# A Transformer block with gated linear attention on one core: every pair of a down pass by sums, with the sums kept over the rounds

## The chip, the cores and the metric

The kernel runs on one core of one Trainium2 chip. The metric is the device time of one execution in microseconds, as the median of several runs. TensorE is called PE below, VectorE DVE, ScalarE ACT, GpSimd POOL, and SyncE, which issues most transfers, SP.

## The reference

One layer for 256 tokens of 2048 values: a mixer with gated linear attention, then a multilayer perceptron (MLP) with a squared ReLU, each ahead of a residual addition and behind an RMS norm, and a last RMS norm.

```python
h = x
h = h + _gla_mixer(_rmsnorm(h, gla_norm), gla_w_in, gla_w_gate_up, gla_b_gate, gla_o_norm, gla_w_out)
h = h + _sq_relu_mlp(_rmsnorm(h, mlp_norm), mlp_w_up, mlp_w_down)
return _rmsnorm(h, final_norm)

def _sq_relu_mlp(h, w_up, w_down):     # w_up 2048 x 8192, w_down 8192 x 2048
    a = jax.nn.relu(h @ w_up)
    return (a * a) @ w_down
```

The change bears on the product with `w_down`, and on how the normed input of the mixer lies in SBUF.

## The kernel before

**Arithmetic.** Every large matrix is float32. A float32 factor is split into a high part (a cast to the type fp32r, done on ACT) and a low part (the difference, done on DVE), and a product is three matmuls: high by high, high by low, low by high. A matmul is 128 x 128 by 256 columns. `halves` (L146) issues those of most stages, `turned` (L180) those in which the weights are the stationary factor.

**Weights.** `weights` loads 128 rows of a weight matrix by SP into a buffer `raw` (three pairs of rows), and splits them into a slot `hi` and a slot `lo` (`parts`, L109 and L110; for `turned` L134 and L135). There are five slots of each, so the splitting runs ahead of PE by at most five slices of 1024 columns.

**Stages.** First come the products of the mixer, the gate, the scores and the output product. Then the MLP, in `ROUNDS` = 4 rounds of 2048 hidden values each: a round has four calls of `up` (q from 0 to 3), which make 512 hidden values each and leave them in `act`, and `down` for the left half of the output columns (half 0) and the right half (half 1). The right half of the last round is done by a closing loop instead, plain, which also ends the kernel.

**The MLP's `up`.** After the 192 matmuls of a call, DVE applies the ReLU (L620), ACT squares (L624), DVE makes four sums of blocks (L627), and both split the result into `act` (L632, L633).

**The MLP's `down`.** A call (a *pass*) has eight pairs of 128 hidden values by 1024 output columns. Of these columns the right 512 are always done plainly, into two banks of PSUM (`plain`). The left 512 columns are seen as 2 x 2 blocks (two halves of the hidden pair by two halves of the columns), and the tokens as two halves as well. A pair *by sums* takes seven block products in place of eight, in Strassen's manner: sums of blocks of `act` (S1 to S4, made in `up`) meet sums of blocks of the weights, made by three operations on DVE (L683) into `work` and split like a third slice `wu`. The seven products go to six half-banks, `b32`, `b74`, `b16`, `b50`. The first pair of a pass (`PLAIN = (0,)`) is done plainly, into the plain banks and parts of the same four. At the end of a pass `take` (L639) adds banks to h, and the combination of the products is made in `ends` (L703, L704) and added to h (L713).

**Order.** PE, DVE and ACT work off their own instruction lists, written out ahead of time by a scheduler that places each instruction by a simulated timeline. So the instructions of a pass's end, of the tail of an up call and of the splitting of the next weights stand mixed on DVE and ACT. Smaller work is put into a list `side` and issued between weight slices by `pump`.

**Where operands lie.** A stationary operand starts 48 values into a block of 64 (`OFF`), a moving one at its start. In each stage that needs it, one row or slice (`EVEN`, `xe`, `gap`) is stored at the other offset. The normed input x, split and turned, lies in two tiles `xth` and `xtl` of 16 rows of 320 values each (`ROW`); behind each row its first 16 values are repeated (`wrap_input`), so that a row can be read from value 16 on when it is the moving operand (`xts`). The tiles that hold the turned h later (`hth`, `htl`) reuse their place.

Of the kernel before, what the change touches and what calls it, by code (L numbers as in the profile page):

```python
# [56 lines left out]
WRAP = 16  # L57
ROW = 320
OFF = 48
EVEN = 5  # L60
# [6 lines left out]
def tile_gla_mlp(ctx, tc, x, xt, cols, w_vg, w_in, w_gate, w_out, w_up, w_down, final_norm, out):  # L67
# [99 lines left out]

    def turned(ah, al, w, c0, even=(0,), acc=None):

        acc = acc or acc_banks(GT // P // 2)  # L170
        for kp in range(KT // 2):
            wh, wl = weights(w[2 * kp * P : 2 * (kp + 1) * P, c0 : c0 + GT].rearrange("(i p) c -> p i c", p=P), 2 * GT, gap=kp in even)
            for i in range(2):
                kt = 2 * kp + i
                for j in range(GT // P):
                    s = slice(j * P, (j + 1) * P)
                    o = acc[j // 2][:, j % 2 * T : (j % 2 + 1) * T]
                    for n, (u, m) in enumerate(((wh, ah), (wh, al), (wl, ah))):

                        nc.tensor.matmul(  # L180
                            o, u[:, i, s], m[:, kt], start=kt == 0 and n == 0 and j % 2 == 0,
                            stop=kt == KT - 1 and n == 2, skip_group_check=True,
                        )
                if kt < KT - 1:
                    pump()
        return acc
# [18 lines left out]
    for _ in range(WARM):  # L205
# [10 lines left out]
    kab = big.tile([P, 2, 8, T], F32, tag="C", name="kab")  # L216
    xth, xtl = (
        big.tile([P, KT * ROW + 64], F32R, tag="A" + i, name="x" + i, bufs=1)[:, OFF : OFF + KT * ROW]
        .rearrange("p (k t) -> p k t", t=ROW)
        for i in "hl"  # L220
    )
    xts = [a[:, :, WRAP : WRAP + T] for a in (xth, xtl)]

    xe = mid.tile([P, 2, P], F32R, tag="xe", name="xe")

    def row_x(kt, t):
        if kt == EVEN and t == 0:
            return [xe[:, i] for i in range(2)]
        return [a[:, kt, t * P : (t + 1) * P] for a in (xth, xtl)]

    def wrap_input(lo, hi):
        k = slice(lo, hi)
        nc.scalar.copy(xth[:, k, T : T + WRAP], xth[:, k, :WRAP].bitcast(F32))
        nc.vector.tensor_copy(xtl[:, k, T : T + WRAP], xtl[:, k, :WRAP].bitcast(F32))

# [12 lines left out]
    def input_tile(kt):  # L248
        if kt in x_loads:
            s = slice(x_done[0], x_loads[kt])  # L250
            nc.sync.dma_start(out=xr[:, s, :], in_=xv[:, s, :])  # L251
            x_done[0] = x_loads[kt]
        if kt == KT - 1:
            wrap_input(0, KT - 2)
        nc.scalar.activation(xth[:, kt, :T], xr[:, kt, :], AF.Copy, scale=g1(kt))  # L255
        nc.vector.scalar_tensor_tensor(
            xtl[:, kt, :T], xr[:, kt, :], g1(kt), xth[:, kt, :T].bitcast(F32), op0=ALU.mult, op1=ALU.subtract
        )
        if kt == EVEN:
            nc.scalar.copy(xe[:, 0], xth[:, kt, :P].bitcast(F32))  # L260
            nc.vector.tensor_copy(xe[:, 1], xtl[:, kt, :P].bitcast(F32))
        return [(0, 512), (512, WMAX)] if kt < FINE else None
# [62 lines left out]
    flush()  # L325
    wrap_input(KT - 2, KT)
    for t in range(NT):
# [89 lines left out]
    for half in range(2):  # L417
        acc = turned(*xts, w_in, KEYW + half * GT, even=(0,) if half else (2,), acc=None if half else [aux_bank(), aux_bank()])
        for b in range(2):
            c0 = 4 * half + 2 * b  # L420
            from_bank(kab[:, 0, c0 : c0 + 2], acc[b])
# [15 lines left out]
    for half in range(2):  # L437
        acc = turned(*xts, w_in, half * GT, even=())
        for b in range(2):
            c0 = 4 * half + 2 * b  # L440
            from_bank(qt[:, c0 : c0 + 2], acc[b])
        side.extend([lambda c=c: extend_q(c) for c in range(4 * half, 4 * half + 4)])
# [131 lines left out]
    add_h(acc, 0)  # L574
    hth, htl = (big.tile([P, KT, T], F32R, tag="A" + i, name="h" + i, bufs=1) for i in "hl")
    turned_h = lambda kt: [a[:, kt, :].rearrange("p (t s) -> p t s", t=NT) for a in (hth, htl)]
    side.extend([lambda: None] + [lambda q=q: turn(h, turned_h, g2, q) for q in range(4)])
# [33 lines left out]
    work = work[:, : 3 * G].rearrange("p (b c) -> p b c", b=3)  # L611
    ends = mid.tile([P, 4, T], F32, tag="db", name="ends")

    def up(r, q, act):
        acc = turned(hth, htl, w_up, r * D + q * GT, even=() if q > 1 or r > 0 and q else (5,) if r == q == 0 else (0,))
        flush()
# [21 lines left out]
    def take(bank, t, lo, n):  # L638
        nc.vector.tensor_tensor(h[:, t, lo : lo + n], bank, h[:, t, lo : lo + n], op=ALU.add)  # L639

    PLAIN = (0,)

    def down(r, half, act):
# [3 lines left out]
        b32, b74 = acc_banks(2) if half == 0 else [aux_bank(), aux_bank()]  # L647
        b16, b50 = acc_banks(2)
        left, right = slice(0, T), slice(T, 2 * T)
        used = set()  # L650

        def product(bank, o, a, w, m, last):

            for i, (x, y) in enumerate(((0, 0), (0, 1), (1, 0))):
                halves(bank[:, o], a[x], w[y][:, m], bank.name not in used, last and i == 2)
                used.add(bank.name)

        for kp in range(KP):
# [5 lines left out]
            ]  # L664
            if kp in PLAIN:
                for i in range(2):
                    wi = weights(w(2 * kp + i), G)
                    blocks(i, wi)
                    product(b32, slice(0, 512), at(A11 + i), wi, slice(0, 512), False)
                    product(b50, right, at(A21 + i), wi, left, False)  # L670
                    product(b74, right, at(A21 + i), wi, right, False)
                    pump()
                continue
            assert not raw_half
# [17 lines left out]
            blocks(1, w1)  # L692
            product(b50, left, at(S1), wu, slice(0, T), last)
            product(b74, left, at(S3), wu, slice(T, 2 * T), last)
# [7 lines left out]

        tt = lambda o, x, y: nc.vector.tensor_tensor(o, x, y, op=ALU.subtract)  # L703
        nc.scalar.copy(ends[:, 1], b16[:, left])  # L704
        tt(ends[:, 3], ends[:, 1], b16[:, right])
        tt(ends[:, 0], b50[:, left], ends[:, 3])
        tt(ends[:, 2], ends[:, 3], b74[:, left])
        take(b32, 0, c0, 512)
        take(b74, 1, c0, 512)
        take(b50[:, right], 1, c0, T)  # L710
        for t in range(NT):
            hv = h[:, t, c0 : c0 + 512].rearrange("p (i s) -> p i s", i=2)
            nc.vector.tensor_tensor(hv, hv, ends[:, 0 : t + 2 : t + 1], op=ALU.add)  # L713

# [105 lines left out]
```

## Time and profile before

| | us |
|---|---|
| median of 3 runs | 1073.5 (1072.7 to 1073.9) |
| the profiled execution, its own time | 1072.98 |
| its span, first to last instruction | 1071.1 |
| busy: PE, DVE, ACT, POOL | 1061.8, 775.1, 574.2, 12.7 |
| granted TensorE clock | 0.998 of full speed |

Times are microseconds from the start of the span. A row of a timeline has start, duration, engine, line, operation, tiles (out<-in), shapes and count, and in brackets the idle time of the engine just before and what ended it. A row of the waits has total, times and longest. A row of the windows has a stretch, its length, the busy time of PE, of PE's weight loading, of DVE, ACT and POOL (each with a count), the granted clock, the share of the DMA engines and GB/s. A row of the groups has line, engine, operation, tiles, shapes and count, then busy time in us, mean ns of one, and idle time before. Matmuls are pipelined, so a matmul is shown as 0.28 us long while the next starts 0.11 us after it.

### The profile page before, as it was taken

What the parts mean: (1) busy time and instruction counts of PE and PEld (TensorE: products, weight loads), DVE (VectorE), ACT (ScalarE), POOL (GpSimd) and SP (SyncE); (2) the same over time, 40 slices, a digit from 0 to 9 for tenths busy, and PEclk for the clock granted to TensorE, in tenths of its full rate; (3) what the DMA queues carried; (4) which work ended last, traced back from release to release, by engine and by line L of the source; (5) the groups of instructions that cost most, each with busy time, mean ns of one, the idle gap of its engine ahead of it and who ended that gap; (6) DMA issues with size and microseconds to landing.
All of it is one profiled execution on the core that took longest, in us unless ns stands there. A gap on an engine that the chain in (4) does not pass through costs nothing.

```text
span 1071.1 us, 21851 instructions
## 1 busy us (share of the span) xinstructions
PE 1061.8 (99%) x9283; PEld 1060.9 (99%) x9283; DVE 775.1 (72%) x1026; ACT 574.2 (54%) x693; POOL 12.7 (1%) x39
## 2 busy tenths in 40 slices
PE   9999999999999999999999999999999999999997
PEld 9999999999999999999999999999999999999997
DVE  7677654656555566789986689987779997678874
ACT  7675444546445455555555446564555554555552
POOL 0000000000000000000000000000000000000000
PEclk9999999999999999999999999999999999999999
DMA  9847654655555555555576555566655656665662
GB/s 341 305 157 233 196 185 137 178 151 179 197 183 183 186 179 183 194 190 201 197 227 204 191 194 173 195 223 210 197 197 179 213 200 215 191 194 189 205 228 79
DMA packets 79569, 210.43 MB, mean 196 GB/s; under 512 B 6720, under 2 KB 7616, under 8 KB 79344
## 3 DMA queue, kind: packets, MB, share of 16 engines
q1 hardware_dynamic: 78512, 206.99, 58.6%
q10 hardware_dynamic: 960, 2.05, 0.5%
q8 instruction: 72, 1.18, 0.4%
q14 instruction: 25, 0.20, 0.1%
HBM read 206.92 MB, written 2.10 MB: 195 GB/s over the span
## 4 chain that ended last, share of the span: by engine, by line
PE 96%; DMA 1%; issue 1%; ACT 0%; DVE 0%; SPq 0%; POOLq 0%; POOL 0%; DVEq 0%; ACTq 0%
PE acc L146 42%; PE acc L180 39%; PE aux L146 12%; PE aux L180 2%; DMA zz<-in_xt 1%; PE aux L525 1%; PE aux L454 1%; DMA raw<-in_w_vg 0%; ACT xh L255 0%; SPq L138 0%; DVE lo L110 0%; ACT hi L109 0%; PE acc L355 0%; SPq L251 0%; DVE hf L779 0%
## 5 line engine op out<-in xcount | busy, mean ns | idle before, releaser
L110 DVE TENSOR_TENSOR lo<-raw,hi 128x1024 fp32r<-128x1024 f32 (+2 forms) x225 | 258.5, 1151 | 123.2 <-ACT hi L109 122.2
L109 ACT CAST hi<-raw 128x1024 fp32r<-128x1024 f32 (+2 forms) x225 | 223.4, 994 | 214.9 <-PE acc L146 115.5
L180 PE MATMUL acc<-hh,hi 128*128 128x256 f32 x1024 | 283.2, 277 | 0.0
L180 PE MATMUL acc<-hh,lo 128*128 128x256 f32 x1024 | 283.1, 276 | 0.0
L180 PE MATMUL acc<-hl,hi 128*128 128x256 f32 x1024 | 283.0, 276 | 0.0
L135 DVE TENSOR_TENSOR lo<-raw,hi 128x1024 fp32r<-128x1024 f32 x160 | 195.7, 1224 | 115.3 <-ACT hi L134 114.6
L134 ACT CAST hi<-raw 128x1024 fp32r<-128x1024 f32 x160 | 168.1, 1051 | 187.5 <-PE acc L180 144.7
L146 PE MATMUL acc<-hi,act 128*128 128x256 f32 x1202 | 217.3, 276 | 0.0
L180 PEld LDWEIGHTS acc<-hh,hi 128*128 128x128 f32 x1024 | 192.3, 188 | 0.0
L180 PEld LDWEIGHTS acc<-hh,lo 128*128 128x128 f32 x1024 | 192.3, 188 | 0.0
L180 PEld LDWEIGHTS acc<-hl,hi 128*128 128x128 f32 x1024 | 192.3, 188 | 0.0
L146 PEld LDWEIGHTS acc<-hi,act 128*128 128x128 f32 x1202 | 180.2, 188 | 0.0
L146 PE MATMUL acc<-lo,act 128*128 128x256 f32 x601 | 142.1, 276 | 0.0
L146 PE MATMUL aux<-hi,act 128*128 128x256 f32 x716 | 135.1, 276 | 0.0
L146 PEld LDWEIGHTS aux<-hi,act 128*128 128x128 f32 x716 | 107.9, 188 | 0.0
L146 PEld LDWEIGHTS acc<-lo,act 128*128 128x128 f32 x601 | 101.9, 188 | 0.0
L146 PE MATMUL acc<-lo,xh 128*128 128x256 f32 x496 | 79.7, 279 | 0.1
L146 PE MATMUL acc<-hi,xh 128*128 128x256 f32 x496 | 78.7, 281 | 0.3 <-ACT hi L109 0.3
L146 PE MATMUL acc<-hi,xl 128*128 128x256 f32 x496 | 78.8, 278 | 0.0
L146 PE MATMUL aux<-lo,act 128*128 128x256 f32 x358 | 76.9, 276 | 0.0
L109 ACT CAST hi<-work 128x1024 fp32r<-128x1024 f32 x49 | 51.7, 1055 | 32.0 <-PE aux L146 12.0
L146 PEld LDWEIGHTS acc<-hi,xh 128*128 128x128 f32 x496 | 66.7, 188 | 0.8 <-ACT hi L109 0.7
(147 smaller groups left out, 1386.1 us busy)
## 6 DMA issues: line engine op xcount, KB each, us to landing
raw<-in_w_up SPq DMA_DIRECT2D x128, 512.0 KB, 4.5
raw<-in_w_down SPq DMA_DIRECT2D x128, 512.0 KB, 4.4
raw<-in_w_in SPq DMA_DIRECT2D x80, 512.0 KB, 4.6
raw<-in_w_out SPq DMA_DIRECT2D x32, 512.0 KB, 4.3
raw<-in_w_vg SPq DMA_DIRECT2D x13, 520.0 KB, 8.0
h<-in_x SPq DMA_DIRECT2D x4, 512.0 KB, 7.1
zz<-in_xt SPq DMA_DIRECT2D x3, 384.0 KB, 7.5
fb<-in_final_norm ACTq DMA_DIRECT2D x1, 1024.0 KB, 7.0
```

What stands on the lines that cost most here:

```text
L109: last_hi[0] = nc.scalar.copy(hi[:, s], raw[:, s])
L110: last_lo[0] = nc.vector.tensor_tensor(lo[:, s], raw[:, s], hi[:, s].bitcast(F32), op=ALU.subtract)
L134: last_hi[0] = nc.scalar.copy(to[0], dst)
L135: last_lo[0] = nc.vector.tensor_tensor(to[1], dst, to[0].bitcast(F32), op=ALU.subtract)
L146: nc.tensor.matmul(o[:, m], x, w[:, m], start=first and c == 0, stop=last, skip_group_check=True)
L180: nc.tensor.matmul(o, u[:, i, s], m[:, kt], start=kt == 0 and n == 0 and j % 2 == 0, stop=kt == KT - 1 and n == 2, skip_group_check=True,)
L454: nc.tensor.matmul(o, kab[:, k[0], c0 + c, k[1] : k[1] + P], q(qt[:, c0 + c]), start=c == 0, stop=c == 1)
L525: nc.tensor.transpose(b[:, i * T + t * P : i * T + (t + 1) * P], src[:, t, kt * P : (kt + 1) * P], ident)
```

## The change

All eight pairs of a pass are done by sums; the branch for the plain pair goes. The bank `b50`, whose right half only the plain pair used, becomes `b5`, half used; likewise the left half of `b74` now holds only the product with the sums S3, and only its right half is added to h.

The combination is no longer made at the end of every pass. Two new tiles `sums`, one for each half of the columns, hold four blocks. In round 0 ACT copies the banks `b16`, `b5` and the left half of `b74` there; in later rounds DVE adds them on. In the last pass of each half (round 3 for half 0, round 2 for half 1) the four blocks are combined once and added to h.

The room for `sums` comes from the input: x's high and low part are each cut into a tile of 12 rows (`CUT`), whose place the turned h takes later, and one of 4 rows, whose place `sums` takes. `turned` now gets a function that gives a row. The wrapped columns are copied for rows 0 to 11 before the last row is made, and for rows 12 to 15 after the stage, where it was 0 to 13 and 14 to 15.

```diff
+CUT = 12
-    def turned(ah, al, w, c0, even=(0,), acc=None):
+    def turned(row, w, c0, even=(0,), acc=None):
...
+                ah, al = row(kt)
...
-                            o, u[:, i, s], m[:, kt], start=kt == 0 and n == 0 and j % 2 == 0,
+                            o, u[:, i, s], m, start=kt == 0 and n == 0 and j % 2 == 0,
...
+    xs = [
+        [
+            big.tile([P, n * ROW + 64], F32R, tag=k + i, name="x" + k, bufs=1)[:, OFF : OFF + n * ROW].rearrange("p (k t) -> p k t", t=ROW)
+            for i in "hl"
+        ]
+        for k, n in (("A", CUT), ("E", KT - CUT))
+    ]
+    def x_row(kt, lo, hi):
+        return [a[:, kt - CUT * (kt >= CUT), lo:hi] for a in xs[kt >= CUT]]
...
         if kt == KT - 1:
-            wrap_input(0, KT - 2)
+            wrap_input(0, 0, CUT)
...
-    wrap_input(KT - 2, KT)
+    wrap_input(1, 0, KT - CUT)
...
+    sums = [big.tile([P, 4, T], F32, tag="E" + i, name="sums", bufs=1) for i in "hl"]
...
-    PLAIN = (0,)
...
-        b16, b50 = acc_banks(2)
+        b16, b5 = acc_banks(2)
...
-            if kp in PLAIN:
-                for i in range(2):
-                    wi = weights(w(2 * kp + i), G)
-                    blocks(i, wi)
-                    product(b32, slice(0, 512), at(A11 + i), wi, slice(0, 512), False)
-                    product(b50, right, at(A21 + i), wi, left, False)
-                    product(b74, right, at(A21 + i), wi, right, False)
-                    pump()
-                continue
...
-        tt = lambda o, x, y: nc.vector.tensor_tensor(o, x, y, op=ALU.subtract)
-        nc.scalar.copy(ends[:, 1], b16[:, left])
-        tt(ends[:, 3], ends[:, 1], b16[:, right])
-        tt(ends[:, 0], b50[:, left], ends[:, 3])
-        tt(ends[:, 2], ends[:, 3], b74[:, left])
+        e = sums[half]
         take(b32, 0, c0, 512)
-        take(b74, 1, c0, 512)
-        take(b50[:, right], 1, c0, T)
+        if r == 0:
+            nc.scalar.copy(e[:, 1:3].rearrange("p b c -> p (b c)"), b16)
+            nc.scalar.copy(e[:, 0], b5[:, left])
+            nc.scalar.copy(e[:, 3], b74[:, left])
+        else:
+            both = e[:, 1:3].rearrange("p b c -> p (b c)")
+            nc.vector.tensor_tensor(both, b16, both, op=ALU.add)
+            nc.vector.tensor_tensor(e[:, 0], b5[:, left], e[:, 0], op=ALU.add)
+            nc.vector.tensor_tensor(e[:, 3], b74[:, left], e[:, 3], op=ALU.add)
+        take(b74[:, right], 1, c0 + T, T)
+        if r < ROUNDS - 1 - half:
+            return
+
+        tt = lambda o, x, y, op: nc.vector.tensor_tensor(e[:, o], e[:, x], e[:, y], op=op)
+        tt(2, 1, 2, ALU.subtract)
+        tt(0, 0, 2, ALU.subtract)
         for t in range(NT):
+            if t == 1:
+                tt(1, 2, 3, ALU.subtract)
+                tt(0, 0, 3, ALU.add)
             hv = h[:, t, c0 : c0 + 512].rearrange("p (i s) -> p i s", i=2)
-            nc.vector.tensor_tensor(hv, hv, ends[:, 0 : t + 2 : t + 1], op=ALU.add)
+            nc.vector.tensor_tensor(hv, hv, e[:, :2], op=ALU.add)
```

More of the change, by code (lines that the diff above doesn't have):

```diff
@@ L216, in tile_gla_mlp @@
     kab = big.tile([P, 2, 8, T], F32, tag="C", name="kab")
[L217 to L222, printed above, removed]
+    xs = [
[7 more added lines that the diff above has]
+        return [a[:, kt - CUT * (kt >= CUT), lo:hi] for a in xs[kt >= CUT]]
+    stream_x = lambda kt: x_row(kt, WRAP, WRAP + T)
     xe = mid.tile([P, 2, P], F32R, tag="xe", name="xe")
@@ L228, in row_x, with wrap_input @@
             return [xe[:, i] for i in range(2)]
[L229 to L234, printed above, removed]
+        return x_row(kt, t * P, (t + 1) * P)
+    def wrap_input(part, lo, hi):
+        h, l = (a[:, lo:hi] for a in xs[part])
+        nc.scalar.copy(h[:, :, T : T + WRAP], h[:, :, :WRAP].bitcast(F32))
+        nc.vector.tensor_copy(l[:, :, T : T + WRAP], l[:, :, :WRAP].bitcast(F32))
     def from_bank(dst, bank):
@@ L253, in input_tile @@
         if kt == KT - 1:
-            wrap_input(0, KT - 2)
[L255 to L258, printed above, removed]
+            wrap_input(0, 0, CUT)
+        h, l = x_row(kt, 0, T)
+        nc.scalar.activation(h, xr[:, kt, :], AF.Copy, scale=g1(kt))
+        nc.vector.scalar_tensor_tensor(l, xr[:, kt, :], g1(kt), h.bitcast(F32), op0=ALU.mult, op1=ALU.subtract)
         if kt == EVEN:
-            nc.scalar.copy(xe[:, 0], xth[:, kt, :P].bitcast(F32))
-            nc.vector.tensor_copy(xe[:, 1], xtl[:, kt, :P].bitcast(F32))
+            nc.scalar.copy(xe[:, 0], h[:, :P].bitcast(F32))
+            nc.vector.tensor_copy(xe[:, 1], l[:, :P].bitcast(F32))
         return [(0, 512), (512, WMAX)] if kt < FINE else None
@@ L417, in tile_gla_mlp @@
     for half in range(2):
-        acc = turned(*xts, w_in, KEYW + half * GT, even=(0,) if half else (2,), acc=None if half else [aux_bank(), aux_bank()])
+        acc = turned(stream_x, w_in, KEYW + half * GT, even=(0,) if half else (2,), acc=None if half else [aux_bank(), aux_bank()])
         for b in range(2):
@@ L437, in tile_gla_mlp @@
     for half in range(2):
-        acc = turned(*xts, w_in, half * GT, even=())
+        acc = turned(stream_x, w_in, half * GT, even=())
         for b in range(2):
@@ L611, in tile_gla_mlp @@
     work = work[:, : 3 * G].rearrange("p (b c) -> p b c", b=3)
-    ends = mid.tile([P, 4, T], F32, tag="db", name="ends")
     def up(r, q, act):
-        acc = turned(hth, htl, w_up, r * D + q * GT, even=() if q > 1 or r > 0 and q else (5,) if r == q == 0 else (0,))
+        acc = turned(lambda kt: (hth[:, kt], htl[:, kt]), w_up, r * D + q * GT, even=() if q > 1 or r > 0 and q else (5,) if r == q == 0 else (0,))
         flush()
@@ L692, in down @@
             blocks(1, w1)
-            product(b50, left, at(S1), wu, slice(0, T), last)
+            product(b5, left, at(S1), wu, slice(0, T), last)
             product(b74, left, at(S3), wu, slice(T, 2 * T), last)
```

## The prediction

> **What bounds the kernel now.** I read the page first: the busy shares and the chain that ended last.
>
> ```profile
> span 1071.1 us, 21851 instructions
> PE 1061.8 (99%) x9283; PEld 1060.9 (99%) x9283; DVE 775.1 (72%) x1026; ACT 574.2 (54%) x693; POOL 12.7 (1%) x39
> PE 96%; DMA 1%; issue 1%; ACT 0%; DVE 0%; SPq 0%; POOLq 0%; POOL 0%; DVEq 0%; ACTq 0%
> ```
>
> TensorE is busy for 99% of the span, and 96% of the chain is its own work. A busy PE could still be one that waits in small pieces, so next came the view of waits, for PE alone. These two rows are its whole answer:
>
> ```profile
> PE aux L206 <- DVE ones L203: 1.0, 1, 1.0
> PE acc L146 <- ACT hi L109: 0.3, 1, 0.3
> ```
>
> Both belong to the start of the kernel. In all four rounds of the MLP, PE waits for nothing. The chain in order of time then gives its pace there, and where each stage lies (start, length, what, count):
>
> ```profile
> 552.66 87.12 PE acc L180 x768
> 639.78 1.36 PE aux L146 x12
> ...
> 643.86 1.70 PE acc L146 x15
> ...
> 722.06 87.12 PE acc L180 x768
> ```
>
> An up stage is 768 matmuls in 87.12 us, 113.4 ns each; in a down pass 12 take 1.36 us and 15 take 1.70 us, 113.3 ns. The two down passes of round 1 lie between 639.78 and 722.06: 82.28 us. By the code a pass is one plain pair of 48 matmuls and seven pairs by sums of 45 each, 363 in all, and 2 x 363 x 113.33 ns is 82.28 us. So the time of this stage is a count of matmuls times one pace. A change moves it by removing matmuls, or by making PE wait or change pace.
>
> **What the change removes.** A pair by sums costs 45 matmuls (24 for the right half, 7 products of 3), a plain pair 48. There are seven down passes (two in rounds 0 to 2, one in round 3) with one plain pair each, so 7 x 3 = 21 matmuls go, at 113.33 ns: **2.38 us**. They are on the path, since PE is.
>
> [...] The trace shows 113.3, and I use that.
>
> **What it adds: work on VectorE just where a pass begins.** The first pair of a pass now needs three split slices of weights instead of two, and the sums that make the third. VectorE (DVE) does the low parts (L110) and the sums (L683). PE's timeline has the first matmul of half 0 of round 1, and DVE's shows what it did around that time:
>
> ```profile
> 639.61 0.39 PE L146 MATMUL aux<-hi,act 128*128 128x256 f32 x2
> ```
>
> ```profile
> 634.56 0.69 DVE L683 TENSOR_TENSOR work<-raw 128x512 f32<-128x512 f32 x1 [0.71 <-DMA raw<-in_w_down]
> ...
> 639.21 1.30 DVE L620 SCALAR_TENSOR_TENSOR su<-acc,work 128x512 f32<-128x512 f32 x2
> 640.83 1.23 DVE L110 TENSOR_TENSOR lo<-work,hi 128x1024 fp32r<-128x1024 f32 x1 [0.33 <-ACT hi L109]
> ...
> 649.28 0.28 DVE L627 TENSOR_TENSOR work<-work 128x128 f32<-128x128 f32 x1
> 649.48 0.68 DVE L683 TENSOR_TENSOR work<-raw 128x512 f32<-128x512 f32 x1
> ...
> 652.76 1.22 DVE L110 TENSOR_TENSOR lo<-raw,hi 128x1024 fp32r<-128x1024 f32 x1
> 653.89 1.22 DVE L110 TENSOR_TENSOR lo<-work,hi 128x1024 fp32r<-128x1024 f32 x1
> 655.03 0.95 DVE L110 TENSOR_TENSOR lo<-raw,hi 128x768 fp32r<-128x768 f32 x1
> 655.90 0.69 DVE L683 TENSOR_TENSOR work<-raw 128x512 f32<-128x512 f32 x1
> ...
> 661.64 1.23 DVE L110 TENSOR_TENSOR lo<-raw,hi 128x1024 fp32r<-128x1024 f32 x1
> ```
>
> From start to next start, an operation on 1024 columns holds DVE for 1.14 us, one on 768 for 0.87, one on 128 for 0.20. The same view at the end of that pass gives the other two sizes, 0.60 for 512 columns and 0.33 for 256:
>
> ```profile
> 685.27 0.41 DVE L703 TENSOR_TENSOR ends<-acc,ends 128x256 f32<-128x256 f32 x1
> 685.60 0.41 DVE L703 TENSOR_TENSOR ends<-ends,acc 128x256 f32<-128x256 f32 x1
> 685.93 0.68 DVE L639 TENSOR_TENSOR h<-acc,h 128x512 f32<-128x512 f32 x1
> 686.53 0.68 DVE L683 TENSOR_TENSOR work<-raw 128x512 f32<-128x512 f32 x1
> ...
> 687.73 0.94 DVE L110 TENSOR_TENSOR lo<-raw,hi 128x768 fp32r<-128x768 f32 x1
> ```
>
> A pair by sums holds DVE for 0.87 + 1.14 + 1.14 + 0.60 + 0.33 + 0.33 = 4.41 us against 45 x 113.33 ns = 5.10 us of PE; a plain pair for 2.28 us against 5.44. So DVE gains 0.69 us on PE in every pair by sums and 3.16 in a plain one. The plain pair is what pays for the work that a pass start brings besides: in half 0 the tail of the last up step, 2 x (0.60 + 0.33 + 0.20 + 0.20 + 1.14) = 4.94 us, in half 1 the end of half 0, with four additions of 512, four operations of 256 and two more of 512: 4.92 us.
>
> How much that leaves is seen as a lead: the end of a slice's low part against the matmul that first wants the slice. From 639.61 on I count 113.33 ns a matmul. The second slice of the sixth pair (after 243 matmuls) is wanted at 667.15 and ready at 662.87: 4.3 us, the usual lead, which the five slots of a slice cap. The second slice of the fourth pair (after 153) is wanted at 656.95 and ready at 653.98: 3.0, the lowest of half 0. In half 1 the first slice of the third pair (after 456) is wanted at 691.29 and ready at 688.67: **2.6 us**, the lowest of all.
>
> **Half 1 afterwards.** The end of half 0 shrinks. In round 0 it is three additions of 512 and one of 256 on DVE, 2.13 us; three copies go to ScalarE (ACT). In rounds 1 and 2 one of 512 and two of 256 are added: 3.39 us. For before, cap less end plus the gains of a plain pair and one by sums is 4.3 - 4.92 + 3.16 + 0.69 = 3.2, where the trace has 2.6; so my balance is 0.6 too kind. For after it gives 4.3 - 2.13 + 1.38 - 0.6 = 2.9 us in round 0 and 4.3 - 3.39 + 1.38 - 0.6 = **1.7 us** in rounds 1 and 2. That is above nothing: PE does not wait.
>
> **Half 0 afterwards.** Nothing shrinks here, and the four slots that are full when the pass begins now cover 15 + 18 + 12 + 15 = 60 matmuls, 6.8 us, instead of 81. The next slice but one, the sums of the second pair, is wanted after 78 matmuls, 8.84 us. By then DVE must do the up tail (4.94) and two splits of 1024 (2.28), plus about 0.5 of idle time as at 640.83, beginning 0.4 before the pass: ready at 7.3, lead 1.5. That holds if the second pair's additions come before the pass, as they do now at 634.56. If they come after it, 1.26 us more, the lead is 0.3. If the scheduler lets the up tail wait, which act's last quarter allows until the seventh pair, it is over 3. I take 1.5, since the row at 634.56 shows the additions early.
>
> **ACT.** It gets one more cast a pass and, in round 0, three copies for one.
>
> ```profile
> 639.78:680.90 41.12, 41.12 (x365) 41.12 (x365) 37.93 (x53) 25.92 (x28) 0.00 (x0) 1.00 0.58 190
> 680.90:722.06 41.16, 41.16 (x366) 41.16 (x365) 38.28 (x52) 23.31 (x25) 0.00 (x0) 1.00 0.62 203
> L704 ACT COPY ends<-acc 128x256 f32<-128x256 f32 x7 | 2.6, 373 | 0.0
> ```
>
> In these stretches (length, then busy time of PE, PEld, DVE, ACT) ACT is busy 23 to 26 of 41 us; some 2 us more, four copies' worth of 256 columns at 373 ns and a cast, find room. DVE at 38 of 41 is the tight one, as reckoned.
>
> **The final combination** (four operations of 256, two of 512: 2.52 us) now stands in one pass of each half. For half 1 an up stage follows, where DVE is idle for over a quarter of the time (first row below, a window as above). For half 0 it is round 3: 5.91 us where there were 4.92, ahead of the closing plain pass. Squares of h are queued on ACT behind it, and casts of weights behind the squares (the view of waits: total, times, longest; then the chain's start of the last down pass, and DVE's timeline):
>
> ```profile
> 552.66:639.78 87.12, 87.12 (x770) 87.12 (x770) 62.47 (x78) 42.37 (x46) 0.00 (x0) 1.00 0.61 201
> ...
> ACT sqf L732 <- DVE h L713: 4.5, 2, 4.3
> ...
> 978.58 1.36 PE aux L146 x12
> ...
> 1028.59 1.23 DVE L110 TENSOR_TENSOR lo<-raw,hi 128x1024 fp32r<-128x1024 f32 x1 [1.21 <-ACT hi L109]
> ```
>
> The closing pass begins 338.80 us (978.58 less 639.78 on the chain) and 363 matmuls after 639.61, at 1019.55. Its sixth row is wanted 120 matmuls on, at 1033.15, and ready at 1029.82: 3.3 us of cover, of which 1.0 goes. Price nothing; without the cover up to 1.0.
>
> ```profile
> L233 ACT CAST xh<-xh 128x224 fp32r<-128x224 f32 (+1 forms) x2 | 0.6, 290 | 0.0
> ```
>
> **The input in two tiles** moves a cut: the wrapped columns are copied for 12 rows and then 4, instead of 14 and 2. The second copy is wanted 144 matmuls into the next stage, 16 us later, which hides it. If a copy did fall on the path, or off it, that is one of 0.29 us either way. I take nothing.
>
> **Sum.** -2.38 us. The profiled execution had a span of 1071.1 us; the median of the runs shown is 1073.5 (1072.7 to 1073.9), and the same 2.38 off it gives **1071.1 us**, -0.22%. About 0.2% (2.15 us) is what a measurement of this kernel can tell from no change, so the forecast lies just beyond that line.
>
> **Rivals.** *First, the slices come late (slower).* Place: the second pair of half 0 in every round, where I reckoned 1.5 us of lead with 0.3 as the low end. It decides once the additions of that pair slip behind the up tail and DVE or ACT idles another 0.3 us: a late cast then holds the low parts behind it, as the squares held casts for 4.3 us above. A wait of 0.5 us alone, four times, costs 2.0 and ends at 1073.1. But PE has a second pace:
>
> ```profile
> 185.94 0.63 PE L146 MATMUL acc<-hi,xh 128*128 128x256 f32 x4
> 186.41 0.63 PE L146 MATMUL acc<-lo,xh 128*128 128x256 f32 x4
> ...
> 192.78 0.40 PE L146 MATMUL acc<-hi,xe 128*128 128x256 f32 x2
> 193.02 0.62 PE L146 MATMUL acc<-hi,xh 128*128 128x256 f32 x4
> 193.47 0.62 PE L146 MATMUL acc<-lo,xh 128*128 128x256 f32 x4
> ```
>
> Four matmuls took 0.47 us (117.5 ns each) before the one row of x that is stored at another offset (xe), 0.45 us after it (112.5 here, 113.3 over a long stretch). The trace doesn't show whether a wait inside a down pass throws PE into the slower pace. If it does, it lasts until the shifted slice of the next up stage: about 640 matmuls x 4.2 ns = 2.7 us a round and 0.5 for the wait, 3.2. In all four rounds that is 12.8, and 1083.9 us; two rounds give 1077.5; one round eats the gain (1071.1 + 3.2 = 1074.3). For it: DVE's 38 of 41 us. Against: a lead of 2.6 today with more work at the end of half 0.
>
> [...]
>
> *Second, the banks.* A pass by sums opens with a product into a bank of its own, where a plain pair opened with the right half. In half 1 this bank must come from half 0, by the first addition to h of its end. If that is queued one operation of 512 too late, PE waits 0.6 us, three times: 1.8, ending at 1072.9, no change. Against it: the order of PE's instructions is settled with those times in view.
>
> *Third, the gain isn't there*, because the new order of the early stages, with x in two tiles, gives some of it back; the 0.29 us above, on one or two copies, puts it at 1071.4 to 1071.7: no change by the bound.
>
> **Chances and range.** The forecast 0.62; around 1071.1 it lies beyond the line at 1071.35 four times in five, so 0.50 faster and 0.12 same. First rival: 0.20 for the slower pace in two rounds or more, 0.08 for waits alone or one round (same). Second 0.06 and third 0.04, both same. In all: faster 0.50, same 0.30, slower 0.20. The range goes from 1070.2 (the forecast less 0.3 for a copy off the path and 0.6 for the spread of the runs) to 1076.0, and leaves out 0.03 below and most of the slower case, 0.17, above.
>
> **What would show it.** 360 matmuls in each down pass and the chain's two passes of a round in 81.6 us instead of 82.28; no row of PE waiting for ACT hi or DVE lo at L146 beyond the early one; DVE's lowest lead near 1.5 us in half 0 and 1.7 in half 1 of rounds 1 and 2. I am wrong if PE shows waits at the second or third pair, or spacings of 117.5 ns inside a down pass.

## The result and the profile after

| | before | after |
|---|---|---|
| median of 17 runs each, us | 1073.17 (1072.70 to 1074.82) | **1070.80** (1069.98 to 1072.87) |
| ratio to before | | 0.9979, 95% interval 0.9972 to 0.9985 |
| the profiled execution, its own time | 1072.98 | 1071.97 |
| its span | 1071.1 | 1070.0 |

The change makes the kernel 0.21% faster, 2.37 us by the medians. Every comparison below has its own runs of the kernel before beside it, with medians of 1073.2 to 1073.3. The profiled executions differ by 1.0 us only, and this needs an explanation too; it lies at the start of the kernel and comes last in this section.

The page of after: the span, the busy engines, and the shares of the chain that ended last.

```profile
span 1070.0 us, 21834 instructions
...
PE 1060.5 (99%) x9262; PEld 1059.9 (99%) x9262; DVE 780.3 (73%) x1039; ACT 579.5 (54%) x699; POOL 12.7 (1%) x39
...
PE 98%; issue 1%; DMA 0%; DVE 0%; ACT 0%; SPq 0%; POOLq 0%; POOL 0%; DVEq 0%; ACTq 0%
```

PE has 9262 matmuls where it had 9283: 21 fewer. The view of waits, for PE alone, again has the start of the kernel and nothing else (total, times, longest):

```profile
PE aux L208 <- DVE ones L205: 1.0, 1, 1.0
PE acc L147 <- ACT hi L110: 0.6, 1, 0.6
```

The chain in order of time, the two up stages on either side of round 1's down passes, and the windows of these two passes and of the up stage before them:

```profile
553.35 87.12 PE acc L182 x768
...
722.07 87.12 PE acc L182 x768
```

```profile
553.35:640.47 87.12, 87.12 (x770) 87.12 (x770) 60.81 (x75) 42.93 (x47) 0.00 (x0) 1.00 0.61 201
640.47:681.26 40.79, 40.79 (x362) 40.79 (x362) 39.68 (x57) 26.29 (x28) 0.00 (x0) 1.00 0.56 194
681.26:722.07 40.81, 40.81 (x363) 40.81 (x362) 37.70 (x50) 24.00 (x24) 0.00 (x0) 1.00 0.61 203
```

The up stage ends at 553.35 + 87.12 = 640.47, so the passes take 722.07 - 640.47 = 81.60 us, where they took 82.28. That is 2 x 360 x 113.33 ns. In the first of them DVE is busy for 39.68 of 40.79 us, and PE still waits for nothing.

Over the whole MLP the same is seen from the first down matmul to the last one. PE's timeline, first and last row of before, then of after:

```profile
470.21 0.39 PE L146 MATMUL aux<-hi,act 128*128 128x256 f32 x2
...
1062.39 0.84 PE L146 MATMUL acc<-room,act 128*128 128x256 f32 x6
```

```profile
471.58 0.28 PE L147 MATMUL acc<-hi,act 128*128 128x256 f32 x1
...
1061.38 0.84 PE L147 MATMUL acc<-room,act 128*128 128x256 f32 x6
```

The last matmul starts five spacings after the last row, at 1062.96 and 1061.95. So this stretch, called the MLP's length from here on, is 592.75 us before and **590.37 us** after: 2.38 less, 21 x 113.33 ns.

**The start.** The MLP of this execution of after began 1.37 us later than before's, so its span fell by 1.1 only. The first matmuls show why. Before, then after:

```profile
5.77 0.54 PE L146 MATMUL acc<-hi,xh 128*128 128x256 f32 x2 [0.28 <-ACT hi L109]
...
8.54 1.12 PE L146 MATMUL acc<-hi,xh 128*128 128x256 f32 x8
9.50 0.40 PE L146 MATMUL acc<-lo,xh 128*128 128x256 f32 x2
```

```profile
6.11 0.81 PE L147 MATMUL acc<-hi,xA 128*128 128x256 f32 x2 [0.63 <-ACT hi L110]
...
7.14 1.49 PE L147 MATMUL acc<-hi,xA 128*128 128x256 f32 x6
8.43 0.63 PE L147 MATMUL acc<-lo,xA 128*128 128x256 f32 x2
...
9.64 0.40 PE L147 MATMUL acc<-hi,xA 128*128 128x256 f32 x2
9.88 0.41 PE L147 MATMUL acc<-lo,xA 128*128 128x256 f32 x2
```

Before, eight matmuls take 9.50 - 8.54 = 0.96 us, 120 ns each. In after, behind a longer wait, six take 8.43 - 7.14 = 1.29 us, 215 ns each, and from 9.64 on two take 0.24. PE runs this execution's first weights at 215 ns a matmul, called half pace from here on, until about 9.5 us. Is that the change, or chance? The tiles alone and the last run below answer it.

### The profile page after: what moved, and what is told of

Its sections match the earlier page's. It is cut to its first block, busy times and chain, and to the rows that moved or that the text cites. A ratio compares the mean times of both kernels' runs of the same rounds, so it can differ in the third digit from the quotient of the medians.

```text
span 1070.0 us, 21834 instructions
## 1 busy us (share of the span) xinstructions
PE 1060.5 (99%) x9262; PEld 1059.9 (99%) x9262; DVE 780.3 (73%) x1039; ACT 579.5 (54%) x699; POOL 12.7 (1%) x39
## 4 chain that ended last, share of the span: by engine, by line
PE 98%; issue 1%; DMA 0%; DVE 0%; ACT 0%; SPq 0%; POOLq 0%; POOL 0%; DVEq 0%; ACTq 0%
PE acc L147 44%; PE acc L182 39%; PE aux L147 12%; PE aux L182 2%; PE aux L533 1%; PE aux L462 1%; DMA raw<-in_w_vg 0%; PE acc L363 0%; DVE hf L789 0%; ACT sqf L742 0%; DVE h L647 0%; ACT hi L110 0%; POOLq L826 0%; POOL rf L297 0%; PE aux L608 0%
## 5 line engine op out<-in xcount | busy, mean ns | idle before, releaser
L147 PE MATMUL acc<-hi,xA 128*128 128x256 f32 x736 | 106.9, 282 | 0.6 <-ACT hi L110 0.6
L147 PEld LDWEIGHTS acc<-hi,xA 128*128 128x128 f32 x736 | 95.2, 190 | 1.1 <-ACT hi L110 0.9
L110 ACT CAST hi<-work 128x1024 fp32r<-128x1024 f32 x56 | 59.1, 1056 | 37.5 <-PE aux L147 13.9
L111 DVE TENSOR_TENSOR lo<-work,hi 128x1024 fp32r<-128x1024 f32 x56 | 68.3, 1220 | 9.4 <-ACT hi L110 7.5
L147 PE MATMUL acc<-lo,xA 128*128 128x256 f32 x368 | 60.1, 281 | 0.0
```

Source lines behind the costliest of these rows:

```text
L110: last_hi[0] = nc.scalar.copy(hi[:, s], raw[:, s])
L111: last_lo[0] = nc.vector.tensor_tensor(lo[:, s], raw[:, s], hi[:, s].bitcast(F32), op=ALU.subtract)
L147: nc.tensor.matmul(o[:, m], x, w[:, m], start=first and c == 0, stop=last, skip_group_check=True)
```

## The experiments

Two theories stand. By the first, time is the count of matmuls, because slices of weights arrive in time; the accumulators, the two tiles and the moved combination cost and bring nothing. By the rival a lead that is used up costs far more than the wait, because PE falls into its slower pace (117.5 ns a matmul where it has 113.3), and the change stands close to that. Line numbers are each kernel's own.

**One part at a time.** From before, all pairs by sums and nothing else:

```diff
-    PLAIN = (0,)
+    PLAIN = ()
...
-        take(b50[:, right], 1, c0, T)
```

> The kernel before with all eight pairs of a pass by sums and the old combination at every pass end (no accumulators, input in one tile). My theory: time is a count of matmuls at 113.33 ns, so this too is 2.38 us faster than before (about 1070.8, ratio 0.9978), as long as no slice is late. By my balance the end of half 0 holds VectorE for 4 x 0.60 + 3 x 0.33 + 2 x 0.60 = 4.59 us, so the lowest lead in half 1 is 4.3 - 4.59 + 1.38 - 0.6 = 0.5 us in every round: no wait, but nearly. The rival says that the accumulators are what makes the eighth pair possible: here the slices come late in half 1 of rounds 0 to 2, PE waits 0.3 to 1 us each, and perhaps changes to 117.5 ns a matmul behind it (1.3 us each): 1072 to 1077.

Measured: 1070.54 us (1070.22 to 1072.18), ratio 0.9973 (0.9963 to 0.9983). The MLP's length is 590.37 us, as with the whole change, and in it PE waits for nothing. What the accumulators would have bought is lead. The lowest one stands where half 1 begins, at the fourth pair's sums (DVE's timeline):

```profile
695.58 1.22 DVE L110 TENSOR_TENSOR lo<-work,hi 128x1024 fp32r<-128x1024 f32 x1 [0.40 <-ACT hi L109]
```

Ready at 696.80, wanted at 698.48, both by the program's order: 1.7 us in rounds 1 and 2, and 1.4 in round 0. I had expected 0.5 by the sum of DVE's work. So three removed matmuls a pass are the whole gain.

Accumulators kept over the rounds, with the plain first pair put back into after's code:

```diff
+    PLAIN = (0,)
...
+            if kp in PLAIN:
...
+                    product(b5, right, at(A21 + i), wi, left, False)
...
+        take(b5[:, right], 1, c0, T)
```

> The changed kernel with the plain first pair put back: accumulators over the rounds and the input in two tiles, but 48 matmuls in the first pair. My theory: as many matmuls as before, so the time of before (1073.2, ratio 0.999 to 1.001), though VectorE has less to do at pass ends and the lowest lead in half 1 rises from 2.6 to about 4. The rival, that part of the gain comes from the shorter pass end, would have it 0.5 us or more faster.

Measured: 1073.55 us (1072.91 to 1075.08), ratio 1.0005 (0.9996 to 1.0014); MLP 592.74 us. By themselves they are worth nothing, as expected.

The input in two tiles alone, with before's down passes (the lines of the change with `xs`, `x_row` and `wrap_input`):

> The kernel before with only the input in two tiles. My theory: no change (1073.2, ratio 0.999 to 1.001); the MLP starts when it did. The rival, which the profile of the changed kernel suggests (its MLP's first down pass began 1.37 us later than before): the tiles cost 1.4 us in the early stages, and this kernel takes 1074.6.

Measured: 1073.33 us (1072.53 to 1074.40), ratio 0.9999 (0.9990 to 1.0008); MLP 592.74 us, and it began at 470.16. The late start of after isn't the tiles'.

**What a lost lead costs.** To after, DVE is given work that nobody reads, where half 1 begins in rounds 1 and 2:

```diff
+LOAD = 6
...
+        if half == 0 and 0 < r < ROUNDS - 1:
+            for _ in range(LOAD):
+                idle = tmp.tile([P, 512], F32, tag="t512", name="idle", bufs=3)
+                nc.vector.tensor_tensor(idle, e[:, 1:3].rearrange("p b c -> p (b c)"), h[:, 0, :512], op=ALU.add)
```

> The changed kernel with six more additions of 128x512 on VectorE (3.6 us, into a tile that nobody reads) at the end of half 0 in rounds 1 and 2. The lowest lead there is 1.9 us in the changed kernel. Theory A, a late slice costs its lateness alone: 1.0 to 1.7 us of waiting in each of the two rounds, matmuls at 113.3 ns behind it, 1073 to 1074. Theory B, a wait also throws PE into the slower pace until the shifted slice of the next up stage: spacings of 117.5 ns from the wait to the end of half 1, some 300 matmuls, 1.3 us more a round, 1075.5 to 1076.8.

Measured: ten runs, three from 1071.4 to 1072.4 and seven from 1077.8 to 1081.2; median 1078.37, ratio 1.0035 (1.0015 to 1.0056, over both kinds). The profiled one took 1078.93. PE's timeline at the fourth pair of half 1, then the chain around and behind it:

```profile
698.78 0.78 PE L148 MATMUL acc<-hi,act 128*128 128x256 f32 x5
699.39 0.34 PE L148 MATMUL acc<-lo,act 128*128 128x256 f32 x1
699.57 0.28 PE L148 MATMUL acc<-hi,act 128*128 128x256 f32 x1
```

```profile
684.77 1.70 PE acc L148 x15
...
700.91 1.77 PE acc L148 x15
...
721.87 86.69 PE acc L183 x764
...
891.55 90.01 PE acc L183 x764
```

Five matmuls take 699.39 - 698.78 = 0.61 us and the next 0.18, where 0.57 and 0.11 would be the pace. That is a wait of 0.1 us in all, far less than the 1.0 to 1.7 that I expected, and too short for a row in the view of waits. By the program's order the slice came 0.73 us late, but the scheduler had put other products first: the first matmul with the low part of these sums is the 535th behind the first of this round's down passes, at 699.39, and in after it is the 529th, at 700.25. Those six matmuls cover 0.68 us. So a lead counted by the program's order says how close a slice is, and a negative one not how long PE will wait. But 15 matmuls behind it take 1.77 us instead of 1.70: **117.8 ns each, not 113.3**. The shifted slice of the next up stage brings the pace back (86.69 us for 764). After the same wait in round 2 it does not: 90.01 us for 764, and so to the end. About 195 matmuls in each of two rounds and 1491 in the last are 1881 x 4.44 ns = 8.4 us, and two waits of 0.1 us make 8.6. The MLP's length is 598.92, 8.55 more than after's. The rival's mechanism, a short wait with the slower pace behind it, is seen here.

The same with three additions in place of six:

```diff
-LOAD = 6
+LOAD = 3
```

> The changed kernel with three extra additions (1.8 us) instead of six in rounds 1 and 2. With six the lowest lead fell from 1.9 to -0.7. By the balance three leave about 0.5: no wait, 113.3 ns all through, 1070.8 as without load. If what counts is VectorE's load as such and not the lead going below nothing, half the cost of six: 1074.

Measured: 1072.23 us (1070.67 to 1072.61), ratio 0.9984 (0.9975 to 0.9994). In the MLP nothing waits, its length is 590.37, and the lowest lead is 1.07 us. With none, three and six additions the lowest lead is 1.89, 1.07 and -0.73. The second three take the 1.8 us that 3 x 0.60 make; the first three meet some slack. The 1.4 us of the median above 1070.8 are not in the MLP: in the profiled execution (1072.26) it began at 471.87, as late as in after, and six of the ten runs lie with it at 1072.2 or more, the other four from 1070.7 to 1071.3.

**The shifted slice.** In rounds 1 to 3 one slice of each first up call is stored at the other offset. Without it:

```diff
-        acc = turned(..., even=() if q > 1 or r > 0 and q else (5,) if r == q == 0 else (0,))
+        acc = turned(..., even=() if q > 1 or r > 0 else (5,) if q == 0 else (0,))
```

> The changed kernel without the shifted slice at the start of the up stages of rounds 1 to 3 and no extra load. As no matmul of the MLP waits there, the pace should stay 113.3 ns all through and 3 x 12 matmuls at 6.7 ns be saved: 0.24 us, 1070.6, ratio to before 0.9975 to 0.998. The rival, that the slice is needed in each round also without waits, gives a slow pace from some place on: 1073 to 1084.

Measured (this edit on after): 1070.25 us (1069.96 to 1071.20), ratio 0.9973 (0.9961 to 0.9984). An up stage on the chain:

```profile
551.58 87.04 PE acc L182 x768
```

That is 0.08 less than 87.12: 12 matmuls of the shifted slice took 120 ns each. The MLP's length is 590.13, three times 0.08 less. The pace stays at 113.3 without the slice, as long as nothing waits. Without it and with the six additions:

> The changed kernel with the six extra additions and, besides, without the shifted slice at the start of the up stages of rounds 1 to 3. Theory B' (a short wait throws PE into 117.8 ns a matmul and only the shifted slice brings it back): the waits of round 1 at about 699 us put all that follows into the slow pace, up stages too: some 3200 matmuls at 4.44 ns, 14 us, so 1084 to 1086 in the runs in which PE waits at all. Rival (the pace comes back by itself with the up stage's other operands): 113.3 ns in the up stages, about 0.9 us a round as in the run with the shifted slice, 1072 to 1074.

Measured: ten runs, two at 1070.2 and 1070.6, eight from 1084.5 to 1086.0; median 1084.78, ratio 1.008 (1.0047 to 1.0114, over both kinds). The profiled execution was one of the two at 1070. PE's timeline has the same short wait, and the chain the pace after it:

```profile
698.97 0.77 PE L148 MATMUL acc<-hi,act 128*128 128x256 f32 x5
699.58 0.33 PE L148 MATMUL acc<-lo,act 128*128 128x256 f32 x1
699.75 0.28 PE L148 MATMUL acc<-hi,act 128*128 128x256 f32 x1
```

```profile
701.04 1.70 PE acc L148 x15
```

Here the same wait left the pace alone, and so did the second one, in round 2 (five matmuls from 867.71 to 868.33). Behind 699.6 there are about 3185 matmuls; at 4.44 ns more each they are 14.1 us, and the two kinds of runs lie 14.4 apart. That the eight ran at 117.8 ns is argued from their time alone, since none of them was profiled. In the profiled executions two of these four short waits, both in the kernel with the shifted slice, were followed by the slower pace; by the times it happens in most executions. The shifted slice ended it once and failed to once; that it limits the damage in general is argued from the medians, 1078.37 with it and 1084.78 without.

The smallest edit that should hold the whole gain, all pairs by sums without the shifted slice (both diffs above, on before):

> The smallest edit that should hold the whole gain: the kernel before with all pairs by sums, the old combination, the input in one tile, and without the shifted slice in the up stages of rounds 1 to 3. By the count 21 x 113.33 ns + 36 x 6.7 ns = 2.62 us less: 1070.6, ratio 0.9976 (0.997 to 0.998), 0.24 us of it seen only in the length of the MLP in the profile (590.1 us from its first down pass to the last matmul). Rival: the lower leads without accumulators (1.4 us) now and then let PE wait, and without the shifted slice the slow pace lasts: some runs at 1076 to 1085.

Measured: 1070.73 us (1070.11 to 1072.37), ratio 0.9977 (0.9968 to 0.9986); MLP 590.13, no wait in it. The expected 0.24 is in the MLP's length and can't be told in the medians.

**More pairs by sums.** If the count is the price, the closing pass has more to give: five of its eight pairs by sums. The last norm's weights then need another place, and `finish`, the last norm's part for half 0, is moved.

```diff
+    SUMS, ROOM = 5, 2
...
+    for kp in range(SUMS):
...
+        product(b16, left, at(A11), w0, right)
...
+    take(b32, 0, G, 512)
+    take(b74, 1, G, 512)
...
+    for kt in range(2 * SUMS, KT):
...
+        held.append((kt, weights(w(kt), G, room=k >= 0 and [room[:, i, k, :] for i in range(2)])))
+    side.extend([lambda t=t, c=c: finish(t, 512 * c, 512) for t in range(NT) for c in range(2)])
```

> The kernel before with all pairs by sums and the old combination, and the first five pairs of the closing pass by sums too (its last three pairs stay plain; the four early squares of h come after the fifth pair). By the count 21 + 15 = 36 matmuls go, 4.08 us: 1069.1, ratio 0.9962, if no slice is late; the end of half 0 in round 3 (4.59 us on VectorE) is now followed by pairs by sums, as in half 1 of the other rounds, where the lowest lead was 1.4 to 1.7 us. Rival: waits in the closing pass and the slow pace behind them for the rest, about 330 matmuls, 1.5 us, or a longer tail behind the last matmul because the combination is late: 1070.5 or more.

Measured: 1072.72 us (1072.12 to 1073.49), ratio 0.9992 (0.9984 to 1.0001). The MLP's length is 589.61, not 588.67. PE's timeline in the closing pass shows the same kind of short wait, and the chain the pace after it:

```profile
1039.16 0.76 PE L146 MATMUL acc<-hi,act 128*128 128x256 f32 x5
1039.75 0.34 PE L146 MATMUL acc<-lo,act 128*128 128x256 f32 x1
1039.93 0.28 PE L146 MATMUL acc<-hi,act 128*128 128x256 f32 x1
```

```profile
1041.27 1.77 PE acc L146 x15
```

192 matmuls at 4.44 ns more are 0.85 us, and the wait 0.1: the 0.94 that were missing. Next, the four calls of `finish` are issued between the splits of the held slices, where DVE had done them among the pairs by sums:

```diff
+    side.extend([lambda t=t, c=c: finish(t, 512 * c, 512) for t in range(NT) for c in range(2)])
     held = []
...
-    side.extend([lambda t=t, c=c: finish(t, 512 * c, 512) for t in range(NT) for c in range(2)])
+        pump()
```

> As the run with the closing pass by sums, with the four early squares of h held back behind the splits of the last six slices. In that run the four products with final_norm held VectorE for 2.4 us in the middle of the closing pass and PE waited 2.0 us behind a cast at 1039, in the slow pace from there. My theory: with these 2.4 us out of the way the lead stays above nothing, 15 more matmuls than in the changed kernel go without a wait, and the time is 1069.0 to 1069.5, ratio 0.996. Rival: five pairs by sums and the end of half 0 are too much for VectorE in the closing pass whatever the order (5 x 4.41 + 4.59 = 26.6 us against 25.5 of PE and 4.3 of lead): still a wait, 1070.5 to 1072.

This expectation rests in part on a misreading: I had put a wait of 2.0 us on ACT's `hi` into the closing pass, where it belonged to the start of the kernel. Measured: 1071.63 us (1071.04 to 1072.61), ratio 0.9985 (0.9976 to 0.9994), short of 1069.0 to 1069.5. The MLP's length is 588.67 = 592.75 - 36 x 113.33 ns, without a wait, so the closing pass now gives all that it should. But the MLP began at 473.6. ACT's timeline of this kernel, then before's row:

```profile
1.23 0.39 ACTq L727 DMA_DIRECT2D fb<-in_final_norm  x1
...
6.00 0.62 ACT L109 CAST hi<-raw 128x512 fp32r<-128x512 f32 x1 [2.34 <-DMA raw<-in_w_vg]
```

```profile
4.02 0.62 ACT L109 CAST hi<-raw 128x512 fp32r<-128x512 f32 x1
```

The second half of the last norm's weights has a place of its own, free from the beginning, so it is loaded at 1.23 us, beside the first weights; their first cast comes 2 us later, at 6.00 us where it was 4.02. PE runs at half pace until about 12.3. The last edits: load them in round 3, and drop the shifted slice.

```diff
+    with tc.issue_after(last_hi[0].ins):
+        for i in range(2):
+            nc.scalar.dma_start(out=fb[i], in_=final_norm[i * G : (i + 1) * G].unsqueeze(0).to_broadcast([P, G]))
```

> The last version with two corrections: the second half of final_norm, which got a place of its own and was therefore loaded in the first 2 us, ahead of the first weights (the first weight matmuls then began about 2 us late and the MLP 3.4 us late), is now loaded in the last pass of round 3; and the shifted slice of rounds 1 to 3 goes. By the count 36 x 113.33 ns + 36 x 6.7 ns = 4.32 us less than before: 1068.9, ratio 0.996 (0.995 to 0.9965), the MLP 588.4 us from its first down pass to the last matmul. Rival: the late start has another cause in this version, and stays: 1071.4.

Measured: 1069.20 us (1068.88 to 1070.31), ratio 0.9961 (0.9947 to 0.9974), MLP 588.43 as expected.

**The start by itself.** Its profiled execution (1069.97) again began the MLP late, at 471.56. Thirteen executions were profiled in all. In those in which PE's last half-pace matmul of the start lay at 6.4 us or before, the MLP began at 469.8 to 470.8 (before and seven others); where it lay near 9.3 to 9.7, at 471.5 to 471.9 (after, the one with three additions, the last one); where at 11 to 12.5, at 472.9 to 473.6 (the two with an early load). In the late ones two matmuls between the fourth and the seventh microsecond had stood 0.91 us apart or more, in the others 0.89 or less. So one more warming product of ones, ahead of the first weights, where PE waits anyway:

```diff
-WARM = 8
+WARM = 9
```

> The best version so far (all pairs by sums, closing pass by sums, late loads, no shifted slice) with nine warming products of ones ahead of the first weights instead of eight: two more matmul records, 0.43 us, placed where PE waits 0.9 us for the second cast of the first weights. What it tests: the kernels' times fall into two groups about 1.4 us apart (before: 24 of 30 runs at 1072.5 to 1073.5, the other 6 from 1073.9 to 1074.9), and in the profiled executions PE starts the weights at 213 ns a matmul and doubles its pace at about 6.0 us or at about 9.5 us, the late ones after longer waits there. Theory 'the pace opens by how busy PE was': less idle time before 6 us, so the pace opens at about 6.0 us in the profiled execution, the MLP begins at 470.0 to 470.3 instead of 471.56, and the runs gather in the lower group: median 1068.9, with at most one of ten above 1069.9. Rival, 'the start varies with the arrival of the first weights alone': the two groups stay, the median is 1069.2, and some three runs of ten lie above 1069.9. From both: the MLP takes 588.43 us as before it, with no wait.

Measured: **1068.56 us** (1068.36 to 1068.92), ratio **0.9955** (0.9941 to 0.9968): the lowest median of all, though the interval overlaps that of the run before it, and five runs within 0.56 us, where the nine of before scatter over 1.8. PE's timeline:

```profile
3.12 1.64 PE L206 MATMUL aux<-ones 128*128 128x128 f32 x9
4.53 0.50 PE L146 MATMUL acc<-hi,xh 128*128 128x256 f32 x2
6.02 0.51 PE L146 MATMUL acc<-hi,xh 128*128 128x256 f32 x2 [0.98 <-ACT hi L109]
...
8.77 1.12 PE L146 MATMUL acc<-hi,xh 128*128 128x256 f32 x8
```

It waits 0.98 us, longer than after did (0.63), and yet runs at the full pace behind it (eight in 0.96 us, as before). The MLP began at 469.98 and took 588.43 us. So the wait alone does not make the late start; the late ones are those in which half pace lasted longer. But the ninth product did not end it here. PE's timeline around 4.3 us, of this kernel and then of after:

```profile
3.98 0.78 PE L206 MATMUL aux<-ones 128*128 128x128 f32 x5
```

```profile
3.98 0.85 PE L208 MATMUL aux<-ones 128*128 128x128 f32 x3
```

A warming product is two matmuls, so the ninth is the last two of the five. The three before it start at 3.98, 4.15 and 4.26, where up to 3.98 they stood 0.213 us apart, and the trace records the full clock from 4.10 us on: it came among the first eight products, earlier than in any other profiled execution. And 88 of the 115 runs of before on record lie in their lower group (below 1073.8), so five early runs in a row come by chance about one time in four ((88/115)^5 = 0.26). These five runs do not tell the warming theory from its rival.

## Why the prediction was right

**The sum.** Removed, 21 matmuls at 113.33 ns: predicted 2.38 us, measured 2.38 in the MLP and 2.37 by the medians. The MLP's length bears out the trace's 113.33: it is 2.38 us less here, and 4.08 less (588.67) for 36 matmuls fewer. The forecast of 1071.1 stood on a median of 1073.5 from three runs; with 1073.17 the same sum gives 1070.8, as measured.

**Half 1.** Predicted leads were 1.7 us in rounds 1 and 2 and 2.9 in round 0; measured, 1.89 and 2.53. The rows of round 1 are the last two below. The second slice of the second pair is wanted after 420 matmuls, at 640.30 + 47.60 = 687.90 (the pass's first matmul starts at 640.30), and ready at 686.01.

**Half 0** is the term that was mis-sized: 1.5 us predicted for the second pair's sums. DVE's timeline:

```profile
637.29 0.69 DVE L680 TENSOR_TENSOR work<-raw 128x512 f32<-128x512 f32 x1
...
643.32 1.22 DVE L111 TENSOR_TENSOR lo<-work,hi 128x1024 fp32r<-128x1024 f32 x1
...
646.47 1.22 DVE L641 TENSOR_TENSOR act<-work,act 128x1024 fp32r<-128x1024 f32 x1
...
647.94 1.22 DVE L111 TENSOR_TENSOR lo<-raw,hi 128x1024 fp32r<-128x1024 f32 x1
...
656.83 1.22 DVE L641 TENSOR_TENSOR act<-work,act 128x1024 fp32r<-128x1024 f32 x1
...
683.54 0.68 DVE L708 TENSOR_TENSOR sums<-acc,sums 128x512 f32<-128x512 f32 x1
...
684.80 1.21 DVE L111 TENSOR_TENSOR lo<-raw,hi 128x1024 fp32r<-128x1024 f32 x1
```

That slice is ready at 644.54 and wanted, 78 matmuls after 640.30, at 649.14: 4.6 us. Its additions came before the pass, at 637.29, as I had taken it. But I had put the whole up tail of 4.94 us ahead of it, and the scheduler let most of the tail wait: the two splits of `act` (L641) stand at 646.47 and 656.83. The lowest lead of half 0 is the third pair's second slice, ready at 649.16 and wanted at 652.20: 3.0 us. The prediction had named this case as "over 3 if the scheduler lets the up tail wait" and not taken it.

**ACT, the combination, the tiles.** Nothing in the MLP waits, so the price of nothing was right; the run with the tiles alone (ratio 0.9999, MLP from 470.16) shows the third rival's term as zero.

**The rivals.** The first rival's mechanism is right and its point of decision was not reached: with 1.89 us to spare nothing waited. Two of its sizes were off. The slower pace costs 4.44 ns a matmul, not 4.2, and it was seen behind a wait of 0.1 us, where 0.5 was reckoned; nor does it surely end at the next shifted slice, so that one such wait late in round 2 cost 7 to 8 us in the profiled execution. The second rival, a bank that comes free too late, would have shown as a wait at the opening of half 1, and there is none.

**Not foreseen:** the 1.4 us by which the start varies from one execution to another, by the times of the runs in before as in after. It is more than half of the gain.

## What to carry to other kernels

Where PE never waited, an edit was worth its count of matmuls times their measured spacing (21 and 36 matmuls, 2.38 and 4.08 us of the MLP). It did not wait with a lowest lead of 1.07 us, and did with one of -0.73: work the leads out slice by slice, and expect a scheduler to move deferrable work out of the way. A wait of 0.1 us can cost not 0.1 us but 4% of the time of the matmuls behind it, as it did behind three of the five profiled here (117.8 ns each, not 113.3), and the view of waits need not show it: compare the chain's time per matmul before and after the place. Look at the first ten microseconds as well: a load given a free place was issued at 1.23 us here, and the first weights came 2 us later; and executions with the same start began the MLP 1.6 us apart (469.99 with six additions, 471.58 in after). Five runs are too few to say that an edit of the start has changed that.

## What was not expected of the hardware

- Two paces inside the MLP, 113.33 and 117.78 ns for the same matmul. In the profiled executions five waits of 0.1 us stand in a down pass or the closing pass: three led to the slower pace (two with six additions, one in the closing pass), two did not (without the shifted slice). By their times 7 of 10 and 8 of 10 runs of the two loaded kernels went that way. What decides it stays open.
- The start. PE begins at half pace, 213 to 215 ns a matmul with the first weights of after, and runs near 118 later. The first record of the full clock in the trace stands at 4.10 us in the last run, at 4.6 to 6.4 in eight executions, at 9.5 to 9.7 in three, and at 4.36 and 12.42 in the two with the early load. In the one with 4.36 (`finish` among the pairs by sums) the clock fell back behind a wait of 2.3 us, from 4.4 to 6.7: half from 7.77, full from 11.18, 3.41 us later. A window between the two, in that kernel:

```profile
7.90:11.10 3.20, 3.20 (x17) 3.20 (x16) 3.15 (x6) 3.17 (x7) 0.00 (x0) 0.50 1.06 418
```

Ahead of the first record the windows show a granted clock of 1.00, where the spacing of the matmuls shows half: between 7.00 and 9.00 us after, whose record stands at 9.52, has 1.00 with 11 matmuls, and before, with its record at 5.87, has 1.00 with 19. There the spacing is to be believed. What sets the moment of the full clock, which differs between executions of one start, no run here shows.
